# Expert retrieval for 64 of 256 tokens by gathered rows and dot products, for 192 by one-hots, with 384-column down products

## The chip, the cores and the metric

One core of a Trainium2 chip runs the whole layer in one launch. The metric is device microseconds from start to end. The engines work side by side: TensorE (PE in the profile; its weight loads are PEld), VectorE (DVE), ScalarE (ACT), GpSimd (POOL) and the DMA queues, of which SP's carries nearly all loads and GpSimd's the indirect ones.

## The reference

A decoder layer of 256 tokens x 1024: modulated RMSNorm, one projection for a retention group and a sparse-attention group, output projection, gated residual; then modulated RMSNorm, an expert retrieval, gated residual, final RMSNorm. The change lies in the retrieval. It has 16384 experts, each one row of `w_down` and one of `w_up` (1024 floats each); every token takes 8 heads x 16 experts:

```
q = (hblk @ w_q).reshape(B, TB, PEER_HEADS, 2, PEER_DHALF)
s = jnp.einsum('btphd,phnd->btphn', q, subkeys).astype(jnp.float32)
v, i = lax.top_k(s, PEER_TOPK)
...
tv, tj = lax.top_k(cand, PEER_TOPK)
eidx = jnp.take_along_axis(cidx, tj, axis=-1)
w = jax.nn.softmax(tv, axis=-1)
u = w_down[eidx]
a = jax.nn.gelu(jnp.einsum('btd,btpkd->btpk', hblk, u).astype(jnp.float32))
vv = w_up[eidx]
return jnp.einsum('btpk,btpkd->btd', (w * a).astype(hblk.dtype), vv)
```

## The kernel before

Everything is float32. For products, each value is cut into two float32r parts: H, ScalarE's rounded copy, and L, VectorE's difference (`split`, line 142). A product of two such values is three matmuls, HH, HL and LH (`mm3`, line 153). All instructions pass through the helper at line 82, so the profile shows that line for nearly every one and the tiles tell them apart.

The retrieval is computed densely: all 16384 activations of all tokens, times a weight that is zero for experts not taken, times all of `w_up`. It works in units of one 512 KB weight block. Sixteen query units (`q_unit`, line 903) make the queries, one later the scores. The 128 down units (`down_unit`, line 1050) each make the activations of 128 experts for 256 tokens: 8 steps over the model width x 3 matmuls of 256 columns, with the weight block as stationary operand; gelu goes to V, an array of 128 experts x 128 units x 256 tokens held in two halves, VL and VH. The 128 up units (`up_units`, line 1090) multiply V by the weight of token and expert where that hasn't been done, split it into a1 and a2, and add 2 token halves x 2 output halves x 3 matmuls of 512 columns into four PSUM banks that stay to the end.

Beside the units two generators run, a few instructions at a time, each paid for by credits: 1.7 a query unit, 1.1 a down unit while `phase` is "top", 1.15 later (CQ, CT, CD); a generator's `yield` names what its piece costs. `top_gen` (line 929) is selection on VectorE: the best 16 of 128 scores for 16 lists, the best 16 of 50 candidate sums for 8 heads, their expert numbers by one-hots, the softmax; first for tokens 128 to 255, then 0 to 127. Then `w_gen` (line 1018) makes the weights of tokens 0 to 127, four tokens a group: two one-hots (row and column of the expert number, fp16), one scaled by the weight in two fp16 parts, 8 matmuls of 128 columns, and a product into V, on VectorE for units already made and a copy on ScalarE for later ones. The weights of tokens 128 to 255 take another way: a table `wd` of 16384 x 128 floats in DRAM is filled with zeros by 8 DMAs of 1 MB (line 886), 128 indirect DMAs of GpSimd add one weight per token into it (`put_weights`, line 1005), and each up unit loads its 64 KB piece, `wt`, and VectorE multiplies it in. When `w_gen` is done and 108 down units are through, up units begin and alternate with the down units left. The last three up units are one step, and then come gate, residual and norm (lines 1225 to 1290). From up unit 28 on, every fourth brings a piece of the last modulation (`gate_unit`), with a 512 KB load.

Order: instructions on an engine run in the order in which a planner put them, by the program's order and its own idea of when operands are there. In the unit loop only the SP queue's order is written out; each selection piece is kept behind the last split. Loads are issued four units ahead but have three buffers (`raw`), so a load waits until the split three before has read its block; H and L have four buffers each.

## Time and profile before

| what | value |
|---|---|
| time, median of 3 runs | 1028.46 us (1022.89 to 1030.41) |
| profiled execution, time | 1026.25 us |
| its span, first to last instruction | 1024.4 us |
| busy: TensorE, its loads | 990.2 us (97%), 870.8 us (85%) |
| busy: VectorE, ScalarE, GpSimd | 742.9 us, 558.2 us, 271.1 us |
| DMA | 216.00 MB, mean 211 GB/s |
| mean granted TensorE clock | 0.993 of full |

Busy time is a mean over stages. Up to 182 us the mixing half of the layer runs, to about 385 us selection with query and down units, to 580 us the one-hots with down units, to 664 us down and up units in turn, to 1001 us up units alone. A matmul's recorded length includes its way through the array: distances between starts tell its cost.

### The profile page before, as it was taken

Reading aid. Unit: us, or ns where it says so; the run is one execution under the profiler, and the core shown is the slowest. Engines: PE = TensorE matmul, PEld = TensorE weight load, DVE = VectorE, ACT = ScalarE, POOL = GpSimd, SP = SyncE. Lnnn points to the kernel's source line nnn. Section 1 sums busy time; section 2 is a strip of 40 time slices with the busy share of each in tenths; the row PEclk is TensorE's granted clock in tenths of the full one; section 3 lists DMA queues with packets and bytes.
Section 4 is the critical chain, followed back from the end, with each engine's and each line's share of the span. In section 5 each row is a group of like instructions: output and inputs, shape, how many; then the busy total and the mean of one; then the engine's idle time right before and its main releaser. Section 6 shows DMA issues by size and latency. Waiting matters only on the chain. (4 is left out here: it accounts for less than half of the span.)

```text
span 1024.4 us, 17290 instructions
## 1 busy us (share of the span) xinstructions
PE 990.2 (97%) x6323; PEld 870.8 (85%) x6323; DVE 742.9 (73%) x1647; ACT 558.2 (54%) x1077; POOL 271.1 (26%) x175
## 2 busy tenths in 40 slices
PE   7999999999999999999999999999999989999995
PEld 6876678999999999999999979988877668777773
DVE  7987988899999997667755455656666656655656
ACT  7544984455544548777754454554444445444443
POOL 1040000200087787787778600000000000000001
PEclk9999999999999999999999999999999999999998
DMA  9979654975577776666676567766778776666662
GB/s 367 409 298 342 209 196 128 356 297 181 175 181 188 183 178 153 142 146 142 139 157 184 134 211 208 206 203 195 251 242 252 244 246 208 200 201 201 205 194 81
DMA packets 94196, 216.00 MB, mean 211 GB/s; under 512 B 27912, under 2 KB 44576, under 8 KB 92704
## 3 DMA queue, kind: packets, MB, share of 16 engines
q1 hardware_dynamic: 73632, 201.99, 61.2%
q0 software_dynamic: 20336, 12.66, 7.6%
q8 instruction: 49, 0.80, 0.3%
q14 instruction: 35, 0.29, 0.1%
q10 hardware_dynamic: 144, 0.26, 0.1%
HBM read 204.31 MB, written 10.56 MB: 210 GB/s over the span
## 5 line engine op out<-in xcount | busy, mean ns | idle before, releaser
L82 ACT ACTIVATE H<-raw 128x1024 fp32r<-128x1024 f32 x284 | 300.2, 1059 | 246.9 <-DMA raw<-in_up_dram 138.2
L82 DVE TENSOR_TENSOR L<-raw,H 128x1024 fp32r<-128x1024 f32 x284 | 346.0, 1219 | 57.1 <-ACT H L82 53.4
L82 PE MATMUL acc<-H,a 128*128 128x512 f32 (+1 forms) x1030 | 325.4, 394 | 8.9 <-DVE a L82 5.7
L1009 POOL DMA_INDIRECT wd<-VL x128 | 241.0, 1883 | 151.1 <-DVE VL L82 95.9
L82 PEld LDWEIGHTS acc<-H,a 128*128 128x128 f32 x1030 | 190.9, 189 | 56.0 <-DVE a L82 10.6
L82 PE MATMUL acc<-L,a 128*128 128x512 f32 (+1 forms) x515 | 203.4, 395 | 6.1 <-DVE L L82 5.7
L82 PE MATMUL acc<-hH,H 128*128 128x256 f32 x704 | 201.8, 287 | 0.0
L82 PE MATMUL acc<-hL,H 128*128 128x256 f32 x704 | 199.6, 284 | 0.0
L82 PE MATMUL acc<-hH,L 128*128 128x256 f32 x704 | 199.2, 283 | 0.0
L82 PEld LDWEIGHTS acc<-hL,H 128*128 128x128 f32 x704 | 134.6, 191 | 0.2 <-DVE hL L82 0.2
L82 PEld LDWEIGHTS acc<-hH,H 128*128 128x128 f32 x704 | 134.6, 192 | 0.0
L82 PEld LDWEIGHTS acc<-hH,L 128*128 128x128 f32 x704 | 134.5, 191 | 0.0
L82 PE MATMUL dn<-hH,H 128*128 128x256 f32 x448 | 127.6, 285 | 0.0
L82 PE MATMUL dn<-hH,L 128*128 128x256 f32 x448 | 126.8, 283 | 0.6 <-DVE L L82 0.6
L82 PE MATMUL dn<-hL,H 128*128 128x256 f32 x448 | 126.8, 283 | 0.0
L82 PEld LDWEIGHTS acc<-L,a 128*128 128x128 f32 x515 | 97.1, 188 | 33.8 <-DVE L L82 14.7
L82 PEld LDWEIGHTS dn<-hH,H 128*128 128x128 f32 x448 | 85.8, 191 | 0.6
L82 PEld LDWEIGHTS dn<-hH,L 128*128 128x128 f32 x448 | 85.6, 191 | 0.8 <-DVE L L82 0.8
L82 PEld LDWEIGHTS dn<-hL,H 128*128 128x128 f32 x448 | 85.6, 191 | 0.6
L82 DVE TENSOR_TENSOR VL<-VL,wt 128x128 f32<-128x128 f32 x64 | 18.6, 291 | 85.5 <-DMA wt<-wd 85.5
L82 DVE TENSOR_TENSOR VH<-VH,wt 128x128 f32<-128x128 f32 x64 | 18.7, 292 | 74.4 <-DMA wt<-wd 74.4
L82 ACT ACTIVATE ow<-o,VL 128x128 f16<-128x128 f16 x128 | 52.4, 578 | 0.0
(345 smaller groups left out, 1212.5 us busy)
## 6 DMA issues: line engine op xcount, KB each, us to landing
raw<-in_down_dram SPq DMA_DIRECT2D x128, 512.0 KB, 3.8
raw<-in_up_dram SPq DMA_DIRECT2D x128, 512.0 KB, 4.0
adaraw<-in_wadaT_dram SPq DMA_DIRECT2D x40, 512.0 KB, 7.0
raw<-in_wq_dram SPq DMA_DIRECT2D x16, 512.0 KB, 8.3
wd<-VL POOLq DMA_DIRECT2D x8, 1024.0 KB, 18.2
wt<-wd SPq DMA_DIRECT2D x128, 64.0 KB, 3.3
raw<-in_win_C_dram SPq DMA_DIRECT2D x12, 512.0 KB, 7.4
rawA<-in_win_A_dram SPq DMA_DIRECT2D x8, 512.0 KB
```

What stands on the lines that cost most here:

```text
L82: i = fn(*a, **kw)
L1009: i = G.indirect_dma_start(wd, bass.IndirectOffsetOnAxis(ap=eid[:, p, k:k + 1], axis=0), exd[:, p, k:k + 1], None, compute_op=ALU.add)
```

## The change

The first 64 tokens leave the dense path, the table in DRAM goes, and the other 192 tokens all get their weights by one-hots.

- Activations lie in two tiles with H and L part side by side (`hT0`, `hT1`), so that one matmul covers both parts of 192 tokens, 384 columns. Down units after selection are "wide": per step one 384-column and one 192-column matmul; ScalarE copies the half of the L part out, VectorE adds the other, and gelu reads the sum. Down units during selection keep three matmuls, of 192 columns.
- V holds 192 tokens. An up unit splits V into interleaved parts (`prepare`, done one up unit ahead) and has 6 matmuls for 128 tokens and 4 for the other 64, whose two parts fill one stationary operand.
- `top_gen` takes tokens 0 to 127 first, and then starts `sparse_gen` for tokens 0 to 63: the 128 partitions hold 64 tokens x 2 halves of their 128 experts, so 64 steps cover all. `h2rep` holds the tokens' rows twice. Each step gathers 128 rows of `w_down` (512 KB, an indirect DMA of GpSimd), and VectorE takes the dot product with `h2rep`. Every 8 steps gelu and weights follow. 28 rows of `w_up` are scaled on ScalarE and added into `accS` by a DMA of GpSimd; the rest are multiplied and added by VectorE after the dots. All rows share five buffers. A down unit pays 0.7 of a step, an up unit 0.45.
- At the end `accS` and the first token half's banks are split and brought together by 8 matmuls with selection matrices.
- `w_gen` has 48 groups for 32, the up units begin when it is done, and the gate pieces start at up unit 36.

```diff
-GATE = 28
+GATE = 36
+TS = 64
+TD = T - TS
+NJ = P // 2
+BLK = 8
+NAX = 2
+BD = 3
+BU = 3
+RD = 0.7
+RU = 0.45
...
-ZC = 2048
-START_UP = 108
...
-    wd2 = mk(dpool, (NT * P, P), F32, "wd")
-    wd = wd2.rearrange("a (b o) -> (a b) o", o=1)
...
+    h2 = [mk(pers, (P, 4, 2, T), F32R, f"hT{n}") for n in range(2)]
+    h2H, h2L = Parts(h2, 0), Parts(h2, 1)
...
+    identR = mk(sp, (P, P), F32R, "identR")
+    S.activation(identR, ident, AF.Copy)
+    h2rep = mk(sp, (P, D), F32, "h2rep")
+    for hf in range(2):
+        b = bank("S")
+        for q in range(4):
+            k = hf * 4 + q
+            for n, a in enumerate((h2H, h2L)):
+                mm(b[:, q * P:(q + 1) * P], a[:, k, :P], identR, n == 0, n == 1)
+        S.activation(h2rep[:TS, hf * 512:(hf + 1) * 512], b[:TS, :], AF.Copy)
+    G.dma_start(h2rep[TS:, :], h2rep[:TS, :])
...
-    zero = vls[:, NT // 2 * T - ZC:NT // 2 * T]
-    wz = wd2.rearrange("(p a) b -> p (a b)", p=P)
-    with tc.issue_after(spill.ins):
-        G.memset(zero, 0.0)
-        for i in range(NT * P // ZC):
-            G.dma_start(wz[:, i * ZC:(i + 1) * ZC], zero)
...
-        s = mk(tk, (P, 2, P), F32, "sco", bufs=8)
...
-        for tt in (1, 0):
+        for tt in range(2):
...
-                yield 0.8
...
+                oh = mk(tk, (P, NCAND, 16), BF, "oh", bufs=1)
+                V.tensor_tensor(oh, ioj, tpf[:, p:p + 1, :].to_broadcast([P, NCAND, 16]), op=ALU.is_equal)
+                oe = mk(tk, (P, NCAND, 16), F32, "oe", bufs=2)
+                V.tensor_tensor(oe, oh, cidx[:, p, :, None].to_broadcast([P, NCAND, 16]), op=ALU.mult)
+                V.tensor_reduce(ev[:, p, :], oe.rearrange("p j k -> p k j"), axis=AX.X, op=ALU.add)
+                yield 2.1
...
-            for p in range(8):
...
-                if tt:
-                    V.tensor_scalar(ev[:, p, :], ev[:, p, :], float(P), tokf, op0=ALU.mult, op1=ALU.add)
-                    V.tensor_copy(eid[:, p, :], ev[:, p, :])
-                    put_weights(p)
-                yield 1.8
-            if tt:
-                continue
...
+            if tt == 0:
+                ew = ex.rearrange("p a b -> p (a b)")
+                V.tensor_copy(idxS[:TS, :], ei[:TS, :NJ])
+                V.tensor_copy(wS[:TS, :], ew[:TS, :NJ])
+                G.dma_start(idxS[TS:, :], ei[:TS, NJ:])
+                last["G"] = G.dma_start(wS[TS:, :], ew[:TS, NJ:])
+                spg.append(sparse_gen())
...
-    sync = mybir.DependencyInfo(mybir.DependencyClass.Sync, mybir.DependencyReason.DATA)
-    placed = []
-    def put_weights(p):
-        group = []
-        for k in range(16):
-            i = G.indirect_dma_start(wd, bass.IndirectOffsetOnAxis(ap=eid[:, p, k:k + 1], axis=0),
-                                     exd[:, p, k:k + 1], None, compute_op=ALU.add)
-            for o in group:
-                tc.declare_no_dep(i.ins, o.ins, reason="a head's places all differ")
-            for o in placed:
-                tc.add_manual_dep(i.ins, o.ins.name, sync, reason="the head before has been added")
-            group.append(i)
-        placed[:] = group
...
+    idxS = mk(sp, (P, NJ), I32, "idxS")
+    wS = mk(sp, (P, NJ), F32, "wS")
+    dotS = mk(sp, (P, NJ), F32, "dotS")
+    cS = mk(sp, (P, NJ), F32, "cS")
+    accS = mk(sp, (P, D), F32, "accS")
+    spg = []
+    def gather(tag, src, j, bufs):
+        r = mk(sp, (P, D), F32, tag, bufs=bufs)
+        G.indirect_dma_start(r, None, src, bass.IndirectOffsetOnAxis(ap=idxS[:, j:j + 1], axis=0))
+        return r
...
+    def sparse_gen():
+        downN = I["downN"]
+        upN = I["up"].rearrange("a b c -> (a b) c")
+        with tc.issue_after(last["G"].ins):
+            G.memset(accS, 0.0)
+        rowD, rowU, sums = {}, {}, []
+        nd, nu, ready = [0], [0], 0
+        def get_d(n):
+            while nd[0] < min(n, NJ):
+                rowD[nd[0]] = gather("row", downN, nd[0], BD + 2)
+                nd[0] += 1
+        def get_u(n):
+            while nu[0] < min(n, NJ):
+                rowU[nu[0]] = gather("row", upN, nu[0], BD + 2)
+                nu[0] += 1
+        def put_sums():
+            while sums:
+                n, r = sums.pop(0)
+                G.dma_start(accS, r, accum_op=ALU.add)
+        def axpy(n, on_dve):
+            r = rowU.pop(n)
+            if on_dve:
+                V.scalar_tensor_tensor(accS, r, cS[:, n:n + 1], accS, op0=ALU.mult, op1=ALU.add)
+            else:
+                S.activation(r, r, AF.Copy, scale=cS[:, n:n + 1])
+                sums.append((n, r))
+        get_d(BD)
+        yield
+        na = 0
+        for j in range(NJ):
+            r = rowD.pop(j)
+            V.scalar_tensor_tensor(r, r, 1.0, h2rep, op0=ALU.mult, op1=ALU.mult, accum_out=dotS[:, j:j + 1])
+            get_d(j + BD)
+            put_sums()
+            if j % BLK == BLK - 1:
+                js = slice(j + 1 - BLK, j + 1)
+                S.activation(cS[:, js], dotS[:, js], AF.Gelu_apprx_tanh)
+                V.tensor_tensor(cS[:, js], cS[:, js], wS[:, js], op=ALU.mult)
+                ready = j + 1
+                get_u(na + 1)
+            elif ready and j % NAX == 0 and na < ready and na in rowU:
+                axpy(na, False)
+                na += 1
+                get_u(na + 1)
+            yield
+        while na < NJ:
+            put_sums()
+            axpy(na, True)
+            na += 1
+            get_u(na + BU)
+            yield
+        put_sums()
...
-        for gi in range(P // 4):
-            t0 = gi * 4
+        for gi in range(TD // 4):
+            v0 = gi * 4
+            t0 = TS + v0
...
-        b = bank("dn" if phase == "up" or n % 3 == 2 else "acc")[:, :T]
+        wide = phase != "top"
+        b = bank("dn" if phase == "up" or n % 3 == 2 else "acc")[:, :2 * TD]
         for k in range(KC):
             ks = slice(k * P, (k + 1) * P)
-            mm3(b, h[:, ks], l[:, ks], h2H[:, k, :], h2L[:, k, :], k == 0, k == KC - 1)
+            if wide:
+                two = [(b.rearrange("p (a b) -> p a b", a=2), h[:, ks], h2[k // 4][:, k % 4, :, TS:]),
+                       (b[:, :TD], l[:, ks], h2H[:, k, TS:])]
+                for n_, o in enumerate(two[::-1] if k else two):
+                    mm(*o, k == 0 and n_ == 0, k == KC - 1 and n_ == 1)
+            else:
+                mm3(b[:, :TD], h[:, ks], l[:, ks], h2H[:, k, TS:], h2L[:, k, TS:], k == 0, k == KC - 1)
...
+        if t0 or wide:
+            g = mk(gt, (P, TD), F32, "g")
+        src = b
+        if wide:
+            S.activation(g, b[:, TD:], AF.Copy)
+            V.tensor_tensor(g, g, b[:, :TD], op=ALU.add)
+            src = g
+        if t0 < TD:
+            S.activation(v[:, t0:], src[:, t0:TD], AF.Gelu_apprx_tanh)
         if t0:
-            g = mk(gt, (P, T), F32, "g")
-            S.activation(g[:, :t0], b[:, :t0], AF.Gelu_apprx_tanh)
+            S.activation(g[:, :t0], src[:, :t0], AF.Gelu_apprx_tanh)
             V.tensor_tensor(v[:, :t0], v[:, :t0], g[:, :t0], op=ALU.mult)
...
+    prepared = {}
+    def prepare(j, ap):
+        if j not in prepared:
+            v = vtile(j)
+            a = mk(ap, (P, TD, 2), F32R, "a", bufs=3)
+            S.activation(a[:, :, 0], v, AF.Copy)
+            V.tensor_tensor(a[:, :, 1], v, f(a[:, :, 0]), op=ALU.subtract)
+            prepared[j] = a
+        return prepared[j]
...
         for j in js:
             h, l = splits.pop(("up", j))
-            v = vtile(j)
-            V.tensor_tensor(v[:, P:], v[:, P:], wts.pop(j), op=ALU.mult)
-            a1 = mk(ap, (P, T), F32R, "a1", bufs=3)
-            a2 = mk(ap, (P, T), F32R, "a2", bufs=3)
-            S.activation(a1, v, AF.Copy)
-            V.tensor_tensor(a2, v, f(a1), op=ALU.subtract)
-            ops.append((j, h, l, a1, a2))
+            ops.append((j, h, l, prepare(j, ap)))
...
         for tt in range(2):
-            tq = slice(tt * P, (tt + 1) * P)
             for hf in range(2):
                 parts = 2 if len(js) > 1 and tt and hf else 1
                 w = 512 // parts
                 for c0 in range(0, 512, w):
-                    for j, h, l, a1, a2 in ops:
-                        for n, (a, b) in enumerate(((a1, h), (a1, l), (a2, h))):
-                            mm(acc_o[tt][hf][:, c0:c0 + w], a[:, tq], b[:, hf * 512 + c0:hf * 512 + c0 + w],
-                               j == 0 and n == 0, j == NUP - 1 and n == 2 and c0 + w == 512)
+                    for j, h, l, a in ops:
+                        cs_ = slice(hf * 512 + c0, hf * 512 + c0 + w)
+                        if tt:
+                            pr = ((a[:, TS:, 0], h), (a[:, TS:, 0], l), (a[:, TS:, 1], h))
+                        else:
+                            a0 = a[:, :TS, :].rearrange("p a b -> p (a b)")
+                            pr = ((a0, h), (a0, l))
+                        for n, (x, b) in enumerate(pr):
+                            mm(acc_o[tt][hf][:, c0:c0 + w], x, b[:, cs_], j == 0 and n == 0,
+                               j == NUP - 1 and n == len(pr) - 1 and c0 + w == 512)
+                if len(js) > 1 and not tt:
+                    dHL = mk(sp, (P, D), F32R, "row", bufs=BD + 2)
+                    dH, dL = dHL[:, :512], dHL[:, 512:]
+                    S.activation(dH, acc_o[0][hf], AF.Copy)
+                    V.tensor_tensor(dL, acc_o[0][hf], f(dH), op=ALU.subtract)
+                    ends.append((dH, dL))
+                if len(js) > 1 and tt and not hf:
+                    for h2, (dH, dL) in enumerate(ends):
+                        b = bank("w")
+                        cs_ = slice(h2 * 512, (h2 + 1) * 512)
+                        for n, (x, y) in enumerate(((sel[:, 0, :], aSH[:, cs_]), (sel[:, 0, :], aSL[:, cs_]),
+                                                    (sel[:, 1, :], dH), (sel[:, 1, :], dL))):
+                            mm(b, x, y, n == 0, n == 3)
+                        acc_t.append(b)
...
-            if u[0] == "up":
-                w = mk(apool, (P, P), F32, "wt2", bufs=2)
-                i_ = Q.dma_start(w, wd2[u[1] * P:(u[1] + 1) * P, :])
-                for o in placed:
-                    tc.add_manual_dep(i_.ins, o.ins.name, sync, reason="all heads have been added")
-                wts[u[1]] = w
...
+            while spg:
+                if next(spg[0], StopIteration) is StopIteration:
+                    spg.pop()
+            sel = mk(apool, (P, 2, P), F32R, "sel", bufs=1)
+            G.memset(f(sel), 0.0)
+            V.tensor_tensor(sel[:, 0, :TS], ident[:, :TS], ident[:, TS:], op=ALU.add)
+            V.tensor_tensor(sel[:, 1, TS:], ident[:, 0::2], ident[:, 1::2], op=ALU.add)
+            aSH = mk(sp, (P, D), F32R, "row", bufs=BD + 2)
+            aSL = mk(sp, (P, D), F32R, "row", bufs=BD + 2)
+            S.activation(aSH, accS, AF.Copy)
+            V.tensor_tensor(aSL, accS, f(aSH), op=ALU.subtract)
...
+            prepare(n, apool)
+            nxt = next((m for w, m in seq[i + 1:] if w == "up"), None)
+            if nxt is not None:
+                prepare(nxt, apool)
             up_units([n], apool)
...
+        if spg:
+            scred += RU if u == "up" else RD
+            while scred >= 1.0 and spg:
+                scred -= 1.0
+                if True:
+                    if next(spg[0], StopIteration) is StopIteration:
+                        spg.pop()
...
-                elif i < 16 + START_UP:
-                    break
...
-        return acc_o[tt][c0 // 512][:, c0 % 512:c0 % 512 + c1 - c0], ys[tt][:, c0:c1], x2s[:, tt, c0:c1], g2s[:, c0:c1]
+        o = acc_o[1] if tt else acc_t
+        return o[c0 // 512][:, c0 % 512:c0 % 512 + c1 - c0], ys[tt][:, c0:c1], x2s[:, tt, c0:c1], g2s[:, c0:c1]
...
+    o["downN"] = g("peer_down")[0]
```

## Rows read from the trace of the kernel before

**Rows 1.** Stretches: start:end, length, each engine's busy us (x instructions), clock, DMA, GB/s.
```profile
0.00:50.00 50.00, 44.07 (x219) 38.10 (x220) 42.79 (x82) 31.50 (x49) 4.69 (x17) 0.97 0.98 387
182.00:385.00 203.00, 203.00 (x1697) 202.79 (x1696) 195.74 (x585) 103.61 (x160) 90.44 (x52) 1.00 0.73 216
385.00:580.00 195.00, 194.92 (x1630) 192.97 (x1629) 121.92 (x258) 134.18 (x338) 154.90 (x85) 1.00 0.66 152
595.00:664.00 69.00, 69.00 (x443) 62.97 (x444) 39.59 (x64) 34.75 (x62) 0.00 (x0) 1.00 0.70 206
725.00:850.00 125.00, 116.26 (x493) 92.46 (x492) 81.92 (x142) 58.41 (x85) 1.75 (x3) 0.99 0.75 243
850.00:1001.00 151.00, 148.92 (x627) 115.33 (x626) 89.84 (x154) 70.27 (x101) 0.00 (x0) 1.00 0.66 201
```
**Rows 2.** Chain of waits, interleaved stage: start us, length us, engine, tile, matmuls.
```profile
595.83 2.86 PE dn L82 x24
598.69 2.75 PE acc L82 x12
```
**Rows 3.** Groups of instructions: shapes, count | busy us, mean ns | idle, releaser.
```profile
L82 ACT ACTIVATE H<-raw 128x1024 fp32r<-128x1024 f32 x284 | 300.2, 1059 | 246.9 <-DMA raw<-in_up_dram 138.2
L82 DVE TENSOR_TENSOR L<-raw,H 128x1024 fp32r<-128x1024 f32 x284 | 346.0, 1219 | 57.1 <-ACT H L82 53.4
L82 DVE SCALAR_TENSOR_TENSOR adaraw<-adaraw,cs 128x1024 f32<-128x1024 f32 x40 | 48.3, 1216 | 0.0
L82 DVE TENSOR_TENSOR VH<-VH,wt 128x128 f32<-128x128 f32 x64 | 18.7, 292 | 74.4 <-DMA wt<-wd 74.4
L82 DVE TENSOR_TENSOR VH<-VH,g 128x128 f32<-128x128 f32 x37 | 10.5, 285 | 0.0
L82 DVE SCALAR_TENSOR_TENSOR VL<-w,VL 128x256 f32<-128x256 f32 x23 | 9.7, 424 | 23.2 <-PE w L82 23.2
```
**Rows 4.** Timeline of VectorE, two places: start us, length us, instruction.
```profile
125.55 1.22 DVE L82 SCALAR_TENSOR_TENSOR adaraw<-adaraw,cs 128x1024 f32<-128x1024 f32 x1
126.70 1.22 DVE L82 TENSOR_TENSOR L<-raw,H 128x1024 fp32r<-128x1024 f32 x1
...
446.34 1.22 DVE L82 TENSOR_TENSOR L<-raw,H 128x1024 fp32r<-128x1024 f32 x1
447.47 0.42 DVE L82 TENSOR_TENSOR o<-VL 128x512 f16<-128x512 f16 x1
447.81 0.42 DVE L82 TENSOR_TENSOR ow<-o,VL 128x512 f16<-128x512 f16 x1
```
**Rows 5.** Timeline of TensorE where 128-column matmuls stand among others.
```profile
188.39 0.60 PE L82 MATMUL w<-subT,qTi 128*128 128x128 f32 x4
188.75 0.36 PE L82 MATMUL acc<-hL,H 128*128 128x256 f32 x1
...
440.50 1.10 PE L82 MATMUL w<-ow,o 128*128 128x128 f16 x8
441.35 0.37 PE L82 MATMUL acc<-hH,H 128*128 128x256 f32 x1
```
**Rows 6.** Groups of instructions on GpSimd that issue DMAs.
```profile
L1009 POOL DMA_INDIRECT wd<-VL x128 | 241.0, 1883 | 151.1 <-DVE VL L82 95.9 <-issue 41.7 <-DVE oe L82 5.0
L886 POOL DMA_DIRECT2D wd<-VL x8 | 4.3, 547 | 0.3 <-POOL VL L884 0.3
```
**Rows 7.** DMA issues at 182:215, 725:850 and overall: count, KB each, us to landing.
```profile
raw<-in_wq_dram SPq DMA_DIRECT2D x8, 512.0 KB, 11.9
raw<-in_up_dram SPq DMA_DIRECT2D x41, 512.0 KB, 4.5
wd<-VL POOLq DMA_INDIRECT x128, 4.2
```
**Rows 8.** Timeline of the end: first product of the result, last matmul.
```profile
1007.65 0.69 DVE L82 TENSOR_TENSOR VL<-acc,VL 128x512 f32<-128x512 f32 x1 [0.59 <-PE acc L82]
...
1013.56 0.28 PE L82 MATMUL acc<-H,a 128*128 128x256 f32 x1
```

More of the change, by code (lines that the diff above doesn't have):

```diff
@@ L145, in split @@
         l = mk(stream, (P, D), F32R, "L", bufs=LB)
-        S.activation(h[:, :n], r[:, :n], AF.Copy)
+        last["H"] = S.activation(h[:, :n], r[:, :n], AF.Copy)
         last["L"] = V.tensor_tensor(l[:, :n], r[:, :n], f(h[:, :n]), op=ALU.subtract)
@@ L188, in rstd_pair @@
         return y, t
+    sp = es.enter_context(tc.tile_pool(name="sp", bufs=1))
     pre = ExitStack()
@@ L306, in x_copy, with __init__, __getitem__ @@
         S.activation(xT[:, 2 * i:2 * i + 2, :], b, AF.Copy)
-    hH = mk(pers, (P, KC, T), F32R, "hH")
-    hL = mk(pers, (P, KC, T), F32R, "hL")
+    class Parts:
+        def __init__(self, tiles, n):
+            self.tiles, self.n = tiles, n
+        def __getitem__(self, at):
+            _, k, c = at
+            if isinstance(k, slice):
+                return self.tiles[k.start // 4][:, :, self.n, c]
+            return self.tiles[k // 4][:, k % 4, self.n, c]
+    hT2 = [mk(pers, (P, 4, 2, T), F32R, f"hT{n}") for n in range(2)]
+    hH, hL = Parts(hT2, 0), Parts(hT2, 1)
     pq = [bank("S"), bank("S")]
@@ L847, in build @@
     pre.close()
-    if stop == "prefix":
-        Q.dma_start(out[0:P, :], f(h2H).rearrange("p a b -> p (a b)")[:, :D])
-        psp["es"].close()
-        es.close()
-        return
     psum_pool("ps3")
@@ L857, in build @@
     vlo = es.enter_context(tc.tile_pool(name="vlo", bufs=1, reuse_waits="tile"))
-    vls = mk(vlo, (P, NT // 2 * T + 832), F32, "VL")
-    VL = vls[:, :NT // 2 * T].rearrange("p (a b) -> p a b", a=NT // 2)
-    small = vls[:, NT // 2 * T:]
+    vls = mk(vlo, (P, NT // 2 * TD + 4 * T + NCAND * 8), F32, "VL")
+    VL = vls[:, :NT // 2 * TD].rearrange("p (a b) -> p a b", a=NT // 2)
+    small = vls[:, NT // 2 * TD:]
     late = ExitStack()
@@ L866, in build @@
     WG = 4
[L867 to L870 removed]
+    tab = small[:, :T].bitcast(F16).rearrange("p (a b) -> p a b", a=2)
+    tabw = small[:, T:T + T // 2].bitcast(F16)
+    tabl = small[:, 2 * T:3 * T]
+    iow = small[:, 3 * T:4 * T].bitcast(F16).rearrange("p (a b) -> p a b", b=WG)
     subT = mk(tk, (P, 16, P), F32, "subT")
     ioi = mk(tk, (P, P, WG), I32, "ioi")
[L874 to L875 removed]
     with tc.issue_after(spill.ins):
@@ L996, in top_gen @@
             S.activation(wt, b[:, 2, :], AF.Copy, scale=WSC)
+            dump(f"e{tt}", ev)
+            dump(f"w{tt}", ex)
             V.tensor_copy(tabw[:, tq], wt)
@@ L1094, in up_units @@
             h, l = splits.pop(("up", j))
-            v = vtile(j)
-            V.tensor_tensor(v[:, P:], v[:, P:], wts.pop(j), op=ALU.mult)
-            a1 = mk(ap, (P, T), F32R, "a1", bufs=3)
-            a2 = mk(ap, (P, T), F32R, "a2", bufs=3)
-            S.activation(a1, v, AF.Copy)
-            V.tensor_tensor(a2, v, f(a1), op=ALU.subtract)
-            ops.append((j, h, l, a1, a2))
+            ops.append((j, h, l, prepare(j, ap)))
         if len(js) > 1:
-            table(AF.Sqrt, f(ops[-1][3])[:, 0:1])
+            table(AF.Sqrt, f(ops[-1][3])[:, 0, 0:1])
         for tt in range(2):
-            tq = slice(tt * P, (tt + 1) * P)
             for hf in range(2):
@@ L1159, in build @@
     credit = 0.0
+    scred = 0.0
     qs = []
@@ L1286 @@
 _NAMES = ["x", "wadaT", "cols", "win_A", "win_B", "win_C", "wout", "pekT", "wk1", "bk1T",
-          "wk2", "pevT", "wv1", "bv1T", "wv2", "wq", "subT", "down", "up", "gfin", "ropeN", "ropeR", "decay", "cmask",
+          "wk2", "pevT", "wv1", "bv1T", "wv2", "wq", "subT", "down", "downN", "up", "gfin", "ropeN", "ropeR", "decay", "cmask",
           "rep", "bmask"]
```

36 lines of the change are left out of this document (8 added, 28 removed).

## The prediction

> **What bounds the kernel now.** I read three views in turn: the stretches (which engine is full in which stage), the chain of waits (what one unit costs there), then the groups of instructions and DMAs. A "unit" is one 512 KB weight block: 16 query units, 128 down, 128 up; each is loaded into one of three raw buffers, split into H (ScalarE) and L (VectorE), and multiplied. From 182 to 580 us TensorE is full: 203.0 of 203.0 and 194.9 of 195.0 us [rows 1]. A down unit is 24 matmuls of 256 columns in 2.86 us, an up unit 12 of 512 in 2.75 us [rows 2], so a matmul takes 119 and 229 ns: about 10 ns + 0.428 ns a column. What the reader should see beside it is VectorE: 195.7 of 203 us in the selection stage, but 121.9 of 195 in the one-hot stage and 89.8 of 151 among the last ups [rows 1]. The first of these has no room left, the later ones have. Among the ups TensorE is not quite full (116.3 of 125, 148.9 of 151 us), and VectorE's product with a table tile waits 74.4 us for its DMA in the VH half alone [rows 3].
>
> **The counts.** Counting the loop's credits (1.7, 1.1, 1.15 a unit against the generators' yields) gives, before: 16 query + 52 down units in selection, 56 in the one-hot stage, 20 interleaved with ups. After: 16 + 47, then 58 (48 one-hot groups for 32), then 23. The gathered part starts after down 26: 14 dots fall into selection, 40 into the one-hot stage, 10 behind it; 28 of the weighted sums go to ScalarE and an adding DMA, 36 to VectorE, all of these behind up 8 or so, ending near up 66.
>
> **The terms.** On TensorE a narrow down unit becomes 24 x (10 + 192 x 0.428) = 2.21 us, a wide one 8 x (174 + 92) = 2.13 us, an up unit 10 x 229 = 2.29 us. Nothing in the rows is 192 wide; a 128-column f32 matmul with its own weight load came every 90 ns (four in 0.36 us), an f16 one every 106 ns (eight in 0.85 us) [rows 5]; so 92 ns is near the floor, and I take it. The Trainium skill says in "TensorE: Matmul & The Clock Gate", section LDWEIGHTS, that a weight load takes its columns over 1.2 GHz, 107 ns here, whatever follows it. By that rule the 192-column matmuls would cost 107 ns and the sum below would be 3 us higher (only the interleaved stage is then TensorE's); the f32 rows speak against it, the f16 rows for it.
>
> On VectorE the next instruction starts before the one ahead has ended, so I use distances: a split 1.13 us, a one-hot instruction 0.34 us, a 1024-wide product with sum 1.15 us (125.55 to 126.70) [rows 4]. The last is the dot's form exactly, by the modulation rows; a weighted sum has the same operands and gets 1.15 us. The wide unit's add (192 columns, one operand in PSUM) lies between 0.285 us (128) and 0.424 us (256) [rows 3]: 0.355, distance 0.27.
>
> **Before selection:** 16 more matmuls for the doubled activations and two copies, 0 to 3 us; 1.5. The 8 MB of zeros go; they are what a query load's 11.9 us stands beside [rows 7], but TensorE was full there, so nothing comes back. Start 183.5.
>
> **Selection, 63 units.** TensorE needs 16 x 2.87 + 47 x 2.21 + scores 6 = 156 us. VectorE: 195.7, less 5 splits (5.6), less index scaling and one-hot work that fell into the stretch (3.7), plus the second table (2) and 14 dots (16) = 205 us. VectorE takes over as the bound: 205 to 215, taken 210. Before, 68 units took 203: the narrow matmul buys nothing here.
>
> **One-hot stage, 58 units.** VectorE: splits 58 x 1.13 = 65.5; 48 groups x (3 x 0.34 + 0.34 + about 0.12) = 71; adds 58 x 0.27 = 15.7; products with g 58 x 0.18 = 10.4; dots 40 x 1.15 = 46; sum 209 us. TensorE: 58 x 2.13 + 48 x 0.85 = 164. ScalarE: 134.2 before [rows 1], half as many groups again, 58 copies of 192 columns and 20 scalings of a row like an H (1.06 us [rows 3]): an estimate of 185 to 195. The DMAs carry 58 blocks and 60 gathers, 62 MB, 285 GB/s, and the 20 adding DMAs; 387 GB/s was reached at the start [rows 1], so they are no bound yet. One engine at 100% that takes turns with one at 90% will not be without gaps; 209 to 235, taken 217. Before, 56 units took 195 to 200.
>
> **Interleaved, 23 down + 19 up.** TensorE 23 x 2.13 + 19 x 2.29 = 92.5; VectorE 92 (42 splits, 10 dots, 15 sums, 23 adds and products, 19 differences). Both full, and the first sum on VectorE waits once for the last adding DMA: 92.5 to 110, taken 99.
>
> **Up alone.** 48 with sums and gate loads: TensorE 110 us; before, 41 such ups took 125 us, 3.05 each, which gives 146 [rows 1]. Now the loop over three raw buffers: landing 4.5 us [rows 7], H 1.06, L 1.22, or 2.3 us a unit; with gathers beside it (1.7 blocks moved a unit against 1.25) landing should be 5 to 6 and L waits behind a sum in half the units: 2.6 to 2.9. Taken 2.67, 128 us. Then 55 without sums: TensorE 126, before's pace (51 in 151 us) 163; the table wait is gone and the loop gives 2.1 to 2.3, so taken 130. This is where the time comes back: 103 ups in 258 us instead of some 309.
>
> **End.** The last three: 38 matmuls of 512 for 36, 8.7 us. The first 128 tokens' result now appears after two more matmul groups instead of first, 3 us before the last matmul instead of 6 (1007.65 and 1013.56 [rows 8]); the 10.8 us behind the last matmul become 11 to 15, taken 13.
>
> **Sum:** 183.5 + 210 + 217 + 99 + 128 + 130 + 8.7 + 13 = 989 us of span, against 1024.4. The profiled run took 1026.25, 1.85 more than its span and 2.2 less than the median of 1028.46; so 991. What covers the cheap parts: gathers lie on GpSimd, 1.88 us each [rows 6] plus 0.3 between them; unknown for 4 KB rows, between the 0.55 us of a plain issue and twice the 1.88; I take 1.88 since the instruction and its 128 indices are the same. At 1.5 gathers a step that is 3.3 us in a step of 5.3 us. If the cover goes, VectorE stands in its queue at the dot, and the next split, and so TensorE, behind it.
>
> **Rivals.**
> *VectorE without gaps* (chance 0.22): every stage at the lower end, 183.5 + 205 + 209 + 92.5 + 110 + 126 + 8.7 + 11 = 946, so 948. For it: 195.7 of 203 us was reached while VectorE was not even the bound. Against: ScalarE at 90% beside it.
> *Ups keep their pace* (0.17): the three raw buffers, not the table tile, held the ups, and gathers lengthen landing. Then 146 + 163 instead of 128 + 130: +51, 1042; half of it 1016. For it: the ups with gate loads lost 7% at 243 GB/s [rows 1]; against: the 74.4 us of table waits, which go.
> *Gathers pace the dots* (0.16), the slower one: five row buffers turn round all gathers, and the one that reuses a summed row waits in GpSimd's queue until the adding DMA has landed; the next dots' gathers stand behind it. Two steps then cost GpSimd 3 x 2.2 + 0.55 + landing. Two steps last 10.7 us, so it decides from a landing of 3.6 us if nothing overlaps; a DMA of that queue landed in 4.2 us [rows 7] with 4-byte elements. At 6 us it is 13.1: 20 pairs of steps x 2.4 and 5 interleaved ones x 5 = +73, 1064. Against: three gathers are ahead, some 16 us.
> That the edits do not do what they say I exclude: the columns are in the code.
>
> **Numbers.** The forecast has 0.45 (970 to 1020). Predicted 991. A measurement of this kernel (1022.9 to 1030.4) cannot tell less than 1%, so faster is below 1018, slower above 1039. Faster: 0.22 + 0.43 of the forecast + a little of the ups' rival (0.05) = 0.70; slower 0.16, of which most is the gathers' rival; same 0.14. Range 948 (all gaps gone) to 1040 (the ups' rival in full); the gathers' rival lies outside.
>
> **What would show it.** Selection and one-hot stage with VectorE above 95% and TensorE below 85%, idle in front of TensorE put down to VectorE's L: steps two and three right. Waits of VectorE for gathered rows over 1 us on most dots: the gathers' rival. Ups in the last stretch at 2.3 to 2.4 us with TensorE over 95%: the return is right; at 2.7 or more with ScalarE's H waiting for raw: the ups' rival. The prediction is wrong in kind if the first two stages together take under 400 us, since then VectorE is not the bound, or if the granted clock, 1.00 in all these rows, falls in TensorE's gaps.

## The result, and the profile after

The changed kernel takes 1198.5 us (median of 4, 1194.2 to 1200.2) against 1027.1 (1022.9 to 1030.4): ratio 1.167 [1.161, 1.172], slower by 17%. The forecast was 991. The profiled execution took 1200.2 us, its span 1198.4.

Where the time went shows in five marks: the end of each stage by the sum of the forecast, in the changed kernel, and in the best version found below (1012 us).

| mark (us from the start) | forecast | changed | best |
|---|---|---|---|
| selection over: first copy of a wide product | 394 | 603 | 418 |
| first split of V for the ups | 610 | 822 | 629 |
| last down product into V | 709 | 924 | 733 |
| last split of V | 967 | 1176 | 985 |
| span | 989 | 1198 | 1008 |

At the first mark the changed kernel is 209 us late, and at every later one 209 to 215. So the loss lies in selection, and all 64 dots lie there too (first at 324 us, last at 600). The page's slices (40 equal ones, 30 us each; busy tenths, clock in tenths) show the stretch, from 318 us on:

```profile
PE   8999999998663533545357789999999999999995
...
DVE  7888887999756544554369999997767666666665
...
PEclk9999999999865555656668899999999999999998
DMA  9886745454589988999888865555777777777772
```

From 350 to 600 us TensorE and VectorE are both about half idle, and the DMA engines are busy (a share of 0.87 to 0.92). Stretches of the changed kernel, columns as in [rows 1]:

```profile
200.00:250.00 50.00, 49.46 (x423) 49.29 (x422) 49.24 (x223) 25.18 (x46) 0.00 (x0) 1.00 0.50 155
400.00:450.00 50.00, 22.26 (x94) 20.57 (x94) 27.05 (x52) 10.17 (x14) 22.30 (x20) 0.53 0.91 260
...
700.00:950.00 250.00, 242.95 (x1500) 225.53 (x1500) 203.48 (x404) 187.28 (x437) 3.59 (x4) 0.98 0.63 198
950.00:1150.00 200.00, 194.03 (x829) 158.33 (x828) 130.50 (x181) 107.98 (x166) 1.67 (x3) 1.00 0.76 249
```

VectorE's queue in the middle of it (the helper is at line 89 in this kernel; start, length, instruction, idle before it and what ended that; `row<-row,h2rep` is a dot, `L<-raw,H` a split):

```profile
412.09 1.22 DVE L89 TENSOR_TENSOR L<-raw,H 128x1024 fp32r<-128x1024 f32 x1
416.02 1.23 DVE L89 SCALAR_TENSOR_TENSOR row<-row,h2rep 128x1024 f32<-128x1024 f32 x1 [2.71 <-DMA row<-in_downN_dram,idxS]
...
422.69 1.23 DVE L89 SCALAR_TENSOR_TENSOR row<-row,h2rep 128x1024 f32<-128x1024 f32 x1 [5.43 <-DMA row<-in_downN_dram,idxS]
...
427.90 1.23 DVE L89 SCALAR_TENSOR_TENSOR row<-row,h2rep 128x1024 f32<-128x1024 f32 x1 [3.98 <-DMA row<-in_downN_dram,idxS]
...
429.05 1.22 DVE L89 TENSOR_TENSOR L<-raw,H 128x1024 fp32r<-128x1024 f32 x1
```

Three dots stand between two splits, and each waits for its gather. In the whole queue 64 dots stand among 24 splits, and then 36 sums among 24 more; the program calls one step for 1.4 units, which would be 91 and 80. TensorE gets a block only when a split comes: one in 17 us here. Selection's own pieces are kept behind the last split, so they come late with it. Waits of the whole kernel (us, times, longest):

```profile
ACT row L89 <- DMA row<-in_up_dram,idxS: 159.7, 25, 16.3
DVE row L89 <- DMA row<-in_downN_dram,idxS: 129.4, 46, 7.0
...
POOL row L1022 <- DVE row L89: 78.3, 34, 5.7
...
PE acc L89 <- DVE L L89: 45.7, 19, 5.7
```

ScalarE's scalings (the first row) stand in front of H in the same way. DMA issues from 350 to 600 us, against [rows 7] (count, KB, median us to landing):

```profile
accS<-row POOLq DMA_DIRECT2D x26, 512.0 KB, 8.1
raw<-in_down_dram SPq DMA_DIRECT2D x21, 512.0 KB, 5.2
row<-in_downN_dram,idxS POOLq DMA_INDIRECT x52, 7.7
row<-in_up_dram,idxS POOLq DMA_INDIRECT x27, 6.6
```

TensorE where it is full, with the 192-column matmuls that [rows 2, 5] could only bound, and then the wide pair:

```profile
261.91 0.39 PE L89 MATMUL dn<-hT,H 128*128 128x192 f32 x2
262.14 0.27 PE L89 MATMUL dn<-hT,L 128*128 128x192 f32 x1
262.25 0.38 PE L89 MATMUL dn<-hT,H 128*128 128x192 f32 x2
...
742.59 0.36 PE L89 MATMUL dn<-hT,H 128*128 128x384 f32 x1
742.79 0.25 PE L89 MATMUL dn<-hT,L 128*128 128x192 f32 x1
742.88 0.37 PE L89 MATMUL dn<-hT,H 128*128 128x384 f32 x1
```

Three narrow ones take 0.34 us (261.91 to 262.25), 112 ns each; a wide pair 0.29 us.

### The profile page after: what moved, and what is told of

It reads as the page before. It is cut to its first block, busy times and chain, and to the rows that moved or that the text cites. A ratio compares the mean times of both kernels' runs of the same rounds, so it can differ in the third digit from the quotient of the medians.

```text
span 1198.4 us, 16232 instructions
## 1 busy us (share of the span) xinstructions
PE 974.3 (81%) x5574; PEld 857.9 (72%) x5574; DVE 880.5 (73%) x1849; ACT 623.7 (52%) x1268; POOL 227.2 (19%) x198
## 3 DMA queue, kind: packets, MB, share of 16 engines
q1 hardware_dynamic: 55200, 193.59, 49.2%
## 4 chain that ended last, share of the span: by engine, by line
PE 26%; DVE 24%; DMA 21%; issue 16%; ACT 6%; POOL 6%; DVEq 0%; SPq 0%; ACTq 0%; POOLq 0%
DVE L L89 9%; PE acc L89 8%; DMA raw<-in_up_dram 8%; DMA row<-in_downN_dram,idxS 6%; PE C L89 5%; POOL row L1022 4%; PE dn L89 4%; ACT H L89 4%; DMA accS<-row 3%; PE O L89 3%; DMA VL<-in_wadaT_dram 3%; PE S L89 3%; PE T L89 2%; DVE accS L89 2%; DVE ti L89 2%
## 5 line engine op out<-in xcount | busy, mean ns | idle before, releaser
L89 PE MATMUL acc<-hT,H 128*128 128x192 f32 (+2 forms) x1072 | 270.3, 341 | 41.6 <-ACT H L89 40.7
L89 PEld LDWEIGHTS acc<-hT,H 128*128 128x128 f32 x1072 | 206.2, 225 | 44.4 <-ACT H L89 43.0
L89 PE MATMUL acc<-hT,L 128*128 128x192 f32 (+1 forms) x688 | 199.5, 299 | 45.7 <-DVE L L89 45.7
L89 PE MATMUL dn<-hT,H 128*128 128x384 f32 (+1 forms) x584 | 168.2, 362 | 23.9 <-ACT H L89 21.2
L89 PEld LDWEIGHTS acc<-hT,L 128*128 128x128 f32 x688 | 151.7, 222 | 49.8 <-DVE L L89 49.8
L89 DVE SCALAR_TENSOR_TENSOR row<-row,h2rep 128x1024 f32<-128x1024 f32 x64 | 78.2, 1224 | 129.9 <-DMA row<-in_downN_dram,idxS 129.4
L89 PE MATMUL dn<-hT,L 128*128 128x192 f32 x464 | 124.9, 285 | 35.0 <-DVE L L89 35.0
L89 PEld LDWEIGHTS dn<-hT,H 128*128 128x128 f32 x584 | 117.9, 223 | 27.3 <-ACT H L89 22.4
L89 PEld LDWEIGHTS dn<-hT,L 128*128 128x128 f32 x464 | 99.2, 215 | 38.1 <-DVE L L89 37.3
L1022 POOL DMA_INDIRECT row<-in_up_dram,idxS x64 | 96.4, 1506 | 90.6 <-DVE row L89 47.2
```

The source lines that it names most:

```text
L89: i = fn(*a, **kw)
L1022: G.indirect_dma_start(r, None, src, bass.IndirectOffsetOnAxis(ap=idxS[:, j:j + 1], axis=0))
```

## The experiments

Three theories. **Order:** dots, scalings and sums stand too densely in the queues of VectorE and ScalarE; splits behind them come late, whether the dot ahead waits or works. **Gathers' pace:** a row buffer's way round, with the adding DMA in it, is slow wherever the dots stand. **Transfers:** the DMA engines are full. Ratios are to the kernel before, run on the same chip.

### The order, and its control

```diff
-                if True:
+                with tc.issue_after(lasts[-4][0].ins), tc.issue_after(lasts[-4][1].ins):
                     if next(spg[0], StopIteration) is StopIteration:
```

`lasts` collects each unit's L and H instruction. A step is then issued behind the split of four units before, so 93 splits stand among the 64 dots. It and its control both have `HB = 3` and `BD + 1` row buffers.

> Each step of the gathered part is issued behind the split of four units before, on VectorE and on ScalarE; one row buffer and one H buffer fewer, so that it fits. In VectorE's queue the 64 dots then stand among 93 splits instead of 24. Order theory (the dots stand too close in VectorE's queue, and the splits behind them wait): VectorE's waits for gathered rows fall from 129 us to under 40, the granted clock stays at 1.00 from 350 to 600 us, and the time is 990 to 1050 us. Gathers' pace theory (a row buffer's way round through gather, dot and adding DMA is slow wherever the dots stand): with four buffers instead of five a dot comes every 5.4 us or more, the waits stay over 100 us, and the time is not under 1090. Transfer theory (the DMA engines are full with gathers and adding DMAs): same bytes over a longer stretch, 1060 to 1130, raw blocks landing in over 6 us.

> The changed kernel with one row buffer and one H buffer fewer and nothing else: the control for the held one. Order theory: 24 splits among the 64 dots as in the changed kernel, so 1180 to 1230 us. Gathers' pace theory: five buffers to four makes the 275 us of the dots 343, so some 1265 us. Transfer theory: 1198 us, as before.

Held 1083.4 us, 1.060 [1.056, 1.064]; control 1206.4, 1.182 [1.178, 1.187]. The hold alone is worth 123 us. VectorE's waits for gathered rows fall to 8.6 us (control 140.0), yet the time is above the order theory's range and inside the transfers', and the clock from 350 to 600 us is 0.75 to 0.95, not the 1.00 of the order theory. What is left shows in a stretch of the held kernel (DMA share 0.93) and in GpSimd's longest wait from 318 to 760 us:

```profile
400.00:450.00 50.00, 42.90 (x292) 40.10 (x293) 38.95 (x80) 32.06 (x70) 16.86 (x17) 0.90 0.93 296
```

```profile
POOL row L1024 <- DMA accS<-row: 158.8, 28, 7.9
```

The gathers stand in GpSimd's queue until an adding DMA has landed, 28 times: my rival's mechanism. The dots hardly wait for it, but ScalarE's scalings wait 44.6 us for their rows, and the chain that ended last runs 8.1% of the span through gathers of `w_up` rows and 3.8% through adding DMAs. The control, with four row buffers for five and one H buffer fewer, loses 8 us to the changed kernel (16 by the ratios), not the 67 that the gathers' pace asked for.

### Sums without adding DMAs, unheld

```diff
-NAX = 2
+NAX = 1000
```

> All 64 weighted sums on VectorE behind the dots: no scaling on ScalarE, no adding DMA, no up gather among the dots. In VectorE's queue only 14 splits stand among the 64 dots (24 in the changed kernel). Order theory: the loss stays, since the splits stand even further behind, though each dot now needs one gather where it needed 1.45: 1120 to 1200 us, granted clock still at about half in part of the dots' stretch. Gathers' pace theory: the five buffers serve the down rows alone, a dot every 2.3 to 3 us, 1080 to 1110. Transfer theory: the adding DMAs go, 1060 or less.

1137.5 us, 1.113 [1.108, 1.119]: the order theory's range, not the transfers' 1060. From 350 to 600 us VectorE is busy 41 to 47 of 50 us, its waits for gathered rows are 30.3 us in all, and TensorE still has 25 to 32 of 50 at a clock of 0.57 to 0.76. So a split is late behind dots and sums that work as well as behind dots that wait.

### Without the gathered part; narrow products alone

```diff
-                spg.append(sparse_gen())
+                G.memset(accS, 0.0)
```

> Leaves out the gathered part: no row of an expert is gathered, no dot, no sum; their result is taken as zero, and all else of the change stands (narrow and wide down products, 192 columns, ten products an up unit, the extra products at the end). What the rest of the change is worth: 183.5 before selection + 200 + 182 (58 wide units at 2.31 us and 48 one-hot groups at 0.85) + 97 + 119 + 128 + 22 = 932, 915 to 960 us, by the order and transfer theories alike. A rival says that the rest of the change is no gain, since the planner orders it badly as well, or the up units keep their old pace: 990 or more.

955.5 us, 0.937 [0.933, 0.942]: all the rest of the change gains 66 us, with the first 64 tokens not paid for. The rival of 990 falls. On top of that, narrow products throughout:

```diff
-        wide = phase != "top"
+        wide = False
```

> Leaves out the gathered part (as in the kernel at 955.5 us), and computes every down product by three narrow products of 192 columns: no 384-column product, no copy of the second half on ScalarE, no add on VectorE. Theory of the matmul's own time (a 192-column product comes every 112 ns, the 384 and 192 pair every 289): 81 units of 24 x 112 = 2.69 us instead of 2.31. Where TensorE sets the pace (58 units of the one-hot stage and 23 interleaved) that is 81 x 0.38 = 31 us at most, less what VectorE gains by 81 adds of 0.27 us: 970 to 990 us. Rival, that VectorE sets the pace there and the wide product costs it more than it saves TensorE: 935 to 955 us.

979.3 us, 0.959 [0.957, 0.961]. The wide product is worth 22 to 24 of the 31 us that matmul times allow.

### What holds the held kernel

The held kernel with, one at a time, all sums on VectorE, three row buffers, and a plain copy for the adding DMA:

```diff
-NAX = 2
+NAX = 1000
...
-BD = 3
+BD = 2
...
-                G.dma_start(accS, r, accum_op=ALU.add)
+                G.dma_start(accS, r)
```

> The held kernel with all 64 weighted sums on VectorE: no scaling on ScalarE and no adding DMA. What is disputed is why the held kernel, at 1083 us, is still 128 us above the one without the gathered part. Transfer theory: the DMA engines were busy 0.95 of the time there, and 28 adding DMAs at some 2.7 us of all engines go (32.1 MB in 111 us of engine time in the changed kernel against 38.4 MB in 109 us without them): the first stretch falls back to VectorE's pace, 1005 to 1035 us, DMA share under 0.85 from 400 to 650. Buffer theory (gathers stand behind the adding DMA in the queue and for want of a row buffer): the same direction, 1000 to 1040, with GpSimd's 159 us of waits for the adding DMA gone. VectorE theory (dots and sums are simply too much work on VectorE): 36 sums become 64, so 28 x 1.28 = 36 us more, 1100 us or above.

> The held kernel with three row buffers instead of four, two down rows asked for ahead instead of three; the same order in VectorE's queue. Buffer theory (a row buffer's way round, gather 6.6 us, dot, scaling and adding DMA 8.4 us, is the pace): the dots' 389 us grow by up to a third, 1150 us or more. Transfer theory (the DMA engines are full at a share of 0.95): the same bytes, the same pace, 1075 to 1110 us. VectorE theory: 1083 us, as with four.

> The held kernel in which the 28 adding DMAs only copy the scaled row over the sum instead of adding it (leaves out the adding of 28 weighted rows), same size, same order. If the adding makes the DMA slow: landing falls from 8.4 us to about that of a raw block under the same load, 5 us or less, the DMA share from 0.95 to under 0.90, and the time to 1030 to 1060. If any DMA from GpSimd's queue lands so late under this load: landing stays at 7 us or more and the time within 10 us of 1083.

Without adding DMAs 1060.3 us, 1.036 [1.033, 1.040]; three buffers 1106.0, 1.083 [1.078, 1.088]; copies 1062.8, 1.040 [1.033, 1.047] (two executions). Three buffers cost 23 us, which is in the transfers' range; the dots' 386 us grow to 405, not by a third as the buffer theory had it. VectorE's own work is not the answer: 28 sums more there, and the kernel is 23 us faster. From 400 to 650 us the copy lands in 6.4 us where the adding DMA takes 8.1, with the DMA share at 0.90 against 0.95: between the two expectations, so the adding is a part of the slow landing and not all of it. But 1060 is in nobody's range. Its stretches show two limits, first VectorE, then, among the ups with sums, neither engine, where ScalarE's H waits for raw blocks (the last row, from 690 to 960 us):

```profile
450.00:500.00 50.00, 46.48 (x311) 41.66 (x310) 48.19 (x113) 41.40 (x121) 9.78 (x10) 0.97 0.77 251
...
800.00:850.00 50.00, 44.35 (x183) 34.17 (x182) 41.04 (x54) 24.55 (x39) 15.10 (x8) 1.00 0.92 331
```

```profile
ACT H L89 <- DMA raw<-in_up_dram: 82.9, 50, 6.0
```

### The add on GpSimd

```diff
-                G.dma_start(accS, r, accum_op=ALU.add)
+                G.tensor_tensor(accS, accS, r, op=ALU.add)
```

The second of the two kernels scales and adds the 36 rows behind the dots in the same way (`axpy(na, False)`).

> The held kernel in which the 28 rows scaled on ScalarE are added to the sum by an instruction of GpSimd instead of by an adding DMA; the other 36 sums stay on VectorE. No row shows the duration of such an add; from one to three VectorE sums, 1.3 to 4 us. Transfer theory: as with all sums on VectorE the DMA share falls under 0.85 from 400 to 650 us, and VectorE has 28 sums less than there (28 x 1.28 = 36 us): 1030 to 1050 us. Rival: GpSimd's adds stand in its queue between the gathers and wait for ScalarE, so that the gathers start later, or they slow VectorE beside them: 1083 us or more, with VectorE's waits for gathered rows back over 30 us or its dots longer than 1.22 us.

> As the one before, with all 64 rows scaled on ScalarE and added on GpSimd: VectorE makes the dots alone. In the up units VectorE loses 36 sums of 1.28 us = 46 us over some 240 us, and ScalarE gains 36 scalings of 1.15. VectorE theory (among the ups VectorE is late next behind the transfers): 15 to 25 us less than the one before, 1010 to 1035. Transfer theory (H waits for raw blocks there, 76 us in the held kernel, and gathers still come): the same as the one before within 10 us.

1096.6 us, 1.075 [1.070, 1.079], and with all 64 there 1115.5, 1.090 [1.086, 1.094]: worse than the adding DMA, and no range of mine held the second. The add's rows in the first of the two, and the one-hot's comparison from 400 to 650 us in it (shortest, median, longest ns):

```profile
L1049 POOL TENSOR_TENSOR accS<-accS,row x28: 2356/2526/3475, 374.8 to 718.8; 128x1024 f32<-128x1024 f32 x28
```

```profile
L89 DVE TENSOR_TENSOR o<-VL x82: 405/415/2650, 431.5 to 649.5; 128x512 f16<-128x512 f16 x82
```

and in the held kernel:

```profile
L89 DVE TENSOR_TENSOR o<-VL x89: 410/421/477, 428.9 to 649.7; 128x512 f16<-128x512 f16 x89
```

The median is the same and the longest is as long as an add: some VectorE instructions stand for the whole of one. One such place in the timeline, GpSimd's add and the comparison beside it:

```profile
465.88 2.40 POOL L1049 TENSOR_TENSOR accS<-accS,row 128x1024 f32<-128x1024 f32 x1 [5.92 <-ACT row L89]
```

```profile
465.91 2.65 DVE L89 TENSOR_TENSOR o<-VL 128x512 f16<-128x512 f16 x1
```

Beside 25 of the 28 adds one VectorE instruction lasts longer than the median of its kind, by 54 us together; the longest dot takes 4.07 us against 1.23 in the held kernel. The other half of that rival, gathers that come late to the dots, isn't there: VectorE waits 6.1 us for them.

### The fourth raw buffer, and the order once more

```diff
-RAW = 3
+RAW = 4
```

on the held kernel with all sums on VectorE, with three row buffers; the same with three raw buffers; the kernel before with four; and the first without the hold.

> The held kernel with all sums on VectorE (1060 us), with four raw buffers for the weight blocks instead of three and three row buffers instead of four. My own rival for the ups, the loop over three raw buffers: H's waits for raw up blocks, 83 us from 690 to 960, fall by half or more, and the ups with sums from 284 us to some 255: 1030 to 1045 us, against it up to 20 us for the missing row buffer. Transfer theory (the engines carry blocks and gathers at a share of 0.87, and a fourth block on its way only lands later): landing of an up block grows from 5.4 to 7 us, no gain, 1055 to 1085.

> The held kernel with all sums on VectorE, three raw buffers and three row buffers: against the same with four raw buffers (1024 us) it isolates the raw buffer, against the same with four row buffers (1060 us) the row buffer. Raw buffer theory: 1055 to 1080 us, the ups with sums at 280 us or more. Row buffer theory (fewer gathers in flight leave the transfers of the blocks more room): 1030 to 1040, most of the 36 us come with the missing row buffer.

> The kernel before with four raw buffers instead of three and nothing else. If its ups were held by the product that waits for its table tile, as I read it (74 us of waits in the VH half): within 1% of 1022 us, 1012 to 1030. If the three raw buffers held them (my rival for the ups): the last 51 ups go from 151 us to 51 x 2.75 = 140 and the 41 ahead of them from 125 to 113, 995 to 1005 us.

> The kernel at 1024 us (four raw buffers, three row buffers, all sums on VectorE) with the hold alone undone: in VectorE's queue 17 splits stand among the 64 dots again, against 93. Order theory: the fourth raw buffer can't help where splits wait behind dots, some 80 to 120 us are lost, 1100 to 1145 us, granted clock under 0.75 from 350 to 550 us. Rival: with four raw buffers and no adding DMA the order matters little any more, 1025 to 1050.

1024.1 us, 1.000 [0.998, 1.003]; 1060.3, 1.035 [1.029, 1.040]; 1021.6, 1.000 [0.998, 1.002]; 1170.1, 1.136 [1.131, 1.141]. The raw buffer gives 35 us here and nothing to the kernel before; the row buffer gives nothing once the adding DMAs are gone. ScalarE's H from 690 to 960 us with three raw and three row buffers, and then with the fourth raw buffer:

```profile
ACT H L89 <- DMA raw<-in_up_dram: 95.6, 57, 3.9
```

```profile
ACT H L89 <- DMA raw<-in_up_dram: 29.1, 24, 2.6
```

Undoing the hold there costs 0.136 of 1024, some 139 us, more than I expected. One stretch with the hold and without:

```profile
400.00:450.00 50.00, 47.18 (x348) 46.06 (x348) 47.35 (x99) 34.28 (x85) 10.56 (x10) 0.93 0.77 253
```

```profile
400.00:450.00 50.00, 22.71 (x104) 21.70 (x104) 35.36 (x73) 5.08 (x10) 21.20 (x20) 0.57 0.75 242
```

Same DMA share, same buffers, and no scaling on ScalarE in either: the order in VectorE's queue is the cause of the large loss.

### A version that beats both

Four raw, four row and four H buffers, all sums on VectorE, held six units back:

```diff
-RAW = 3
+RAW = 4
...
-PRAW = 3
+PRAW = 2
...
-                if True:
+                with tc.issue_after(lasts[-6][0].ins), tc.issue_after(lasts[-6][1].ins):
```

and two variations of density, `RU = 0.6` on the kernel at 1024, and `RD = 0.6` with `lasts[-10]` on this one:

> The held kernel with all sums on VectorE, four raw and four row buffers, four H buffers, each step behind the split of six units before, and two buffers instead of three for the raw blocks of the early stages. Row buffer theory: the fourth row buffer hides the gathers' 5 to 7 us better, 1005 to 1020 us. VectorE and transfer theory (VectorE 48 of 50 us busy from 400 to 650 us, the DMA engines 0.92 from 690 on): nothing to win, 1018 to 1035.

> The kernel at 1024 us with 0.6 instead of 0.45 steps of the gathered part per up unit: 105 splits between the last dot and the last sum instead of 133. Transfer theory: the DMA engines at 0.92 have no room, the sums' gathers come closer together, the ups under them slow down and the ones behind them speed up: the same within 6 us. Order theory: a denser queue puts VectorE's sums ahead of splits again: 5 to 15 us slower.

> The kernel at 1012 us with the steps of the gathered part thinner and looser: 0.6 instead of 0.7 a unit among the down units, each behind the split of ten units before instead of six. VectorE theory: it is full from 400 to 650 us (48 of 50), and some 13 dots move behind it: 1002 to 1012. Transfer theory: they move to where the DMA engines stand at 0.92 to 0.97, and cost there what they save: 1008 to 1020.

1011.9 us, 0.991 [0.988, 0.993]: faster than the kernel before by 0.9%, a small gain but clear of noise, and than the changed one by 187 us. Against the kernel at 1024 four things differ, and which of them gave the 12 us isn't shown. The gathered part costs it 56 us over the kernel without, most of the 66 that the rest of the change gains. The denser sums take 1029.5, 1.007 [1.005, 1.010], 5 us more or 7 by the ratios, on the border of the two expectations; the thinner dots 1017.4, 0.989 [0.985, 0.992], by the ratios no difference, which decides nothing. The best kernel's stretches show what is left: VectorE, then the DMA engines.

```profile
400.00:600.00 200.00, 180.24 (x1245) 170.49 (x1245) 193.28 (x444) 156.16 (x430) 41.99 (x39) 0.95 0.76 250
750.00:950.00 200.00, 193.59 (x822) 156.85 (x821) 172.03 (x219) 110.98 (x166) 67.69 (x40) 0.99 0.94 346
```

## Why the prediction was wrong

**The counts failed.** "14 dots fall into selection, 40 into the one-hot stage, 10 behind it", and the sums "behind up 8 or so, ending near up 66": I read where the program calls a step and took it for the queue. Selection pieces are kept behind the last split, steps of the gathered part are not, so the planner pulled them forward, to 2.7 dots a split. All 64 dots fell into selection, which ended at 603 us instead of 394, and all sums were done at 718 us, a hundred before the first up. My own sentence on a lost cover, that VectorE stands at the dot and the next split behind it, describes what happened; I had priced the cover by program order. Held to that order and without adding DMAs, the kernels make their first split of V at 629 to 634 us against 610 forecast. From the control to the best kernel the steps are, by their times: the hold 123 us, the adding DMAs 23, the raw buffer 36, the last four changes 12.

**What held, by luck.** Behind selection the kernel keeps the forecast's pace, but with other work than the forecast's: the one-hot stage took 219 us for 217 with 36 sums in it where 40 dots were forecast, much the same on VectorE, and the interleaved stage 102 for 99 without any dot or sum. The forecast's sum also counts only 125 of the 128 up units (19, 48, 55 and 3), some 7 us too little.

**The matmul terms.** Narrow: 24 x 112 ns = 2.69 us for 2.21; wide 2.31 for 2.13; an up unit 2.29 as taken (218 matmuls in the full 50 us from 1100). Of my two rows the fp16 one, 106 ns, was the right neighbour, and the f32 row I hadn't read to its end: the matmul behind the four starts at 188.75 us, but the next only 0.20 us later where its neighbours come every 0.12, which makes the four 0.44 us, 110 ns each (the fp16 row, read the same way, gives 117).

```profile
188.95 0.28 PE L82 MATMUL acc<-hH,L 128*128 128x256 f32 x1
189.07 0.28 PE L82 MATMUL acc<-hH,H 128*128 128x256 f32 x1
```

The Trainium skill's rule in "TensorE: Matmul & The Clock Gate", section LDWEIGHTS, that a weight load takes its columns over 1.2 GHz (107 ns), agrees with 112 within 5%, and not with the 92 that I took. For 81 wide units 0.18 us each is 15 us at most, where TensorE sets the pace; in the changed kernel's half-idle stretch it doesn't. In selection, before the gathers, TensorE was full beside VectorE (49.5 and 49.2 of 50 us from 200 to 250), where I had it below 85%.

**VectorE and GpSimd.** The dot's 1.15 us holds (427.90 to 429.05 above); a sum comes every 1.20. A gather takes GpSimd 1.0 us in the median for a `w_down` row and 1.5 for a `w_up` row, not the 1.88 that I took, so its issue was covered; its landing, 7.7 us for a `w_down` row, is what the dots waited for. "VectorE above 95%" in the one-hot stage holds only where the order is mended (193 of 200 us).

**Transfers.** "No bound yet", said of the one-hot stage by 387 GB/s at the start, failed with the adding DMAs: a share of 0.93 at 296 GB/s in the held kernel. Without them it holds there, 0.76 at 250 in the best kernel; that one's DMA engines are full later, among the ups, 0.94 at 346.

**The return among the ups** was right: 252 us for the ups alone, 258 forecast. But it was right without sums beside them, which had gone early, so that is luck too. With them and three raw buffers the two held kernels without adding DMAs take 284 us, halfway to my rival's 309, and 261 with a fourth raw buffer and nothing else changed. The rival's other half, that the three raw buffers held the ups of the kernel before, fell (1.000 with four).

**Gathers pace the dots** (chance 0.16, 1064 us) named the adding DMA's landing as what decides: 8.1 us, above its 3.6. It shows in the held kernel, where taking the adding DMAs away is worth 23 us, not 73. It came on top of the order.

**VectorE without gaps** (948 us) is seen nowhere; even without the gathered part the kernel takes 955. **The clock:** I had put "wrong in kind if the granted clock falls": it fell to 0.53, nearly always the lower of its levels, 1.2 GHz. I read it as a consequence, since TensorE was idle over half of that stretch even so (22 of 50 us busy); no run separates the two.

The first 100 us after the gathers begin are slow in every held kernel (300 to 400 us: TensorE 34.5 to 42.4 of 50, clock 0.73 to 0.90). From 350 on VectorE is the bound (47.7 to 48.9 of 50). Before that, in the held kernel at 1060 us, VectorE stands 6.2 us at the first dot, whose gathered rows are not there yet, with two splits behind it, and H waits 12.3 us for its next raw block:

```profile
326.88 1.23 DVE L89 SCALAR_TENSOR_TENSOR row<-row,h2rep 128x1024 f32<-128x1024 f32 x1 [6.18 <-DMA row<-in_downN_dram,idxS]
```

```profile
336.40 1.06 ACT L89 ACTIVATE H<-raw 128x1024 fp32r<-128x1024 f32 x1 [12.28 <-DMA raw<-in_down_dram]
```

What stays open is how much of that time is the clock's.

## What to carry to other kernels

Read the order of an engine's queue, not of the program, before counting how work spreads; where a planner decides, a side task without a hold can be pulled in front of the work that feeds the busiest engine, and 123 and 139 us hung on one such hold here. Work that a busy engine must do for others goes ahead of work that can wait. A buffer count that is worth nothing in one kernel (1.000) can be worth 35 us in another, here in one whose loads share the DMA engines with gathers.

## What the runs showed of the hardware

- A GpSimd add of 128x1024 took 2.36 us at the least and 2.53 in the median, and a VectorE instruction beside it could stand for its whole length (a comparison 2650 ns, median 415; one beside 25 of 28 adds). The Trainium skill says in "SBUF — State Buffer", section Who interferes with whom, that a VectorE instruction with two SBUF inputs and a GpSimd one that reads SBUF exclude each other for a whole instruction; the rows of the section on that add agree.
- An adding DMA of 512 KB within SBUF landed in 8.1 us (changed kernel from 350 to 600 us, held kernel from 400 to 650), a copy of the same size in the held kernel in 6.4, a raw block beside that copy in 5.7.
- In the changed kernel the granted clock was 1.00 with TensorE busy 49.5 of 50 us, and 0.53 to 0.60 in the five stretches from 350 to 600 us, with 20 to 26.
